# Low parts of all weights by subtraction on VectorE, and a shorter interval between the modulation's multiply-adds

## The chip, the cores and the metric

The kernel runs on one core of one Trainium2 chip. The metric is the device time of one execution in microseconds (us). Below, TensorE is also PE, VectorE DVE, ScalarE ACT, GpSimd POOL and SyncE SP, as the profile's rows have them.

## The reference, cut to what matters

One transformer layer on 512 tokens of width 2048, all in float32. What is computed must be seen only in outline:

```python
mod = silu(c) @ w_ada + b_ada                    # 6 vectors of 2048: sh1 sc1 gt1 sh2 sc2 gt2
h = rms_norm(x, norm1_g) * (1 + sc1) + sh1
proj = h @ w_in                                  # attention q k v, index q k w, recurrence r k v and low-rank parts
mixed = concat(sparse_attention(...), recurrence(...)) @ w_out
x = x + gt1 * mixed
h2 = rms_norm(x, norm2_g) * (1 + sc2) + sh2
ffn = (silu(h2 @ w_ffn_gate) * (h2 @ w_ffn_up)) @ w_ffn_down
x = x + gt2 * ffn
```

The modulation `mod` is a vector times a 2048 x 12288 matrix. `sh1` and `sc1` are needed at the start, `gt1` at the end of the output projection, `sh2` and `sc2` at the second norm, `gt2` at the end.

## The kernel before

**Split matmuls.** A matrix product is made of three matmuls in the float32r format: a weight tile is split into `whi`, its rounded value, and `wlo`, what the rounding left, and so are the activations; the products hi x hi, lo x hi and hi x lo are added up in PSUM. Three matmuls with 512 columns are one step, so TensorE has three passes over all weights.

**Jobs.** The weights stream in as jobs (lines 231 to 292). A job is a tile `wraw` of 128 x 1024 (512 KB), loaded by SyncE into one of 3 buffers by `issue_to`, which is called for the job three ahead. `split_to` makes `whi` and `wlo` of its two halves of 128 x 512, in 4 buffers each, so two jobs' worth: at the start of a job the halves of this job and the next are asked for, and from its middle one more. `run_jobs` writes the job's matmuls and yields after every third.

**The two ways of splitting.** `split` (line 196) has ScalarE cast the half to `whi`, and VectorE subtract it from the raw half to give `wlo`. In the stage between the first projection blocks and the output projection, where `state["mid"]` is set (line 1496), every second half goes another way (lines 259 to 263): ScalarE casts it, ScalarE writes the negated `whi` into `wlo`, and GpSimd issues a DMA that reads the same weights once more from HBM and adds them to `wlo`.

**What sets the order.** The order of the instructions on each engine is made when the program is built. Streams (generators) for the recurrence's preparation (`prep_stream`), the triangular solves (`solve(0)` on GpSimd, `solve(1)` on VectorE), the recurrence (`scan`), its end (`post_stream`), the sparse attention's index and top-k (`idx_stream`), the attention heads (`head_stream`) and the modulation (`ada_stream`) run beside the jobs; `drive` steps each of them after every third matmul. A planner's clock `clk`, built from rough costs of each instruction (lines 73 to 86), tells a stream when to go on: `until` waits on the planner's TensorE clock until a tile should be ready, and `room(engine, limit)` until the planned queue of an engine is no longer than the limit ahead of TensorE, in planned microseconds. Nothing of that clock is in the program: only the order that came out of it is.

**The modulation.** `ada_stream` (lines 974 to 1008) goes through 16 blocks (4 each for `gt1`, `sh2`, `sc2`, `gt2`) of 16 chunks. A chunk is a tile `wad` of 128 x 512 (256 KB), loaded by SyncE three chunks ahead. The first chunk of a block is scaled on ScalarE, the others are multiplied and added on VectorE (`scalar_tensor_tensor`, line 1006). At the end of a block VectorE transposes and reduces it to `part`, and after four blocks TensorE spreads `part` into `pc`. Chunks of the first twelve blocks, 192, follow one another by at least `PACE` = 4.2 of the planner's microseconds (lines 997 to 1000); the last four blocks start with the feed-forward. `norm2` (line 1349) writes nothing until the first twelve blocks are in the order: it waits for `done["ada"]` to be 12. Then come the sum of squares `pst`, the inverse root `rr`, its transpose `prb` and the first tiles of `h2`.

Of the kernel before, what the change touches and what calls it, by code (L numbers as in the profile page):

```python
# [8 lines left out]
F32 = mybir.dt.float32  # L9
F32R = mybir.dt.float32r  # L10
I32 = mybir.dt.int32
AF = mybir.ActivationFunctionType
OP = mybir.AluOpType
# [10 lines left out]
PAIRS = 8  # L24
# [24 lines left out]
def layer_kernel(ctx, tc, x, c, positions, w_ada, b_ada, norm1_g, w_in, q_norm_g, k_norm_g,  # L49
# [38 lines left out]
    class Queue:  # L88
# [3 lines left out]
        def __getattr__(self, op):  # L92
# [3 lines left out]
            def call(*args, **kw):  # L96
# [26 lines left out]
                if key2 != "pe":  # L123
                    for v in vals[1:]:
                        if nm(v) in psread:
# [4 lines left out]
    PE, V, A, P, SP = (Queue(e, k) for e, k in ((nc.tensor, "pe"), (nc.vector, "dve"), (nc.scalar, "act"),  # L130
                                                (nc.gpsimd, "pool"), (nc.sync, "dma")))

    def now():
        return clk["pe"]

    SLACK = 0.5
    PACE, PACE2 = 4.2, 3.0

    def until(*aps):

        t = max(ready.get(nm(a), 0.0) for a in aps) + SLACK
        while now() < t:
            yield

    def room(key="dve", lim=3.0):
        while clk[key] - now() > lim:
            yield
# [25 lines left out]
    def G(name="g", dt=F32):  # L173
        return gpool.tile([128, 512], dt, name=name, tag="g")
# [21 lines left out]
    def split(hi, lo, src, eng=None):  # L196
        A.copy(hi, src)
        (eng or V).tensor_tensor(lo, src, hi.bitcast(F32), op=OP.subtract)
# [34 lines left out]
    state = {"issued": 0, "split": 0, "mid": False, "ffn": False}  # L233
# [16 lines left out]
    def split_to(n):  # L250
        while state["split"] < min(n, len(subs)):
            j, u = subs[state["split"]]
            if j["i"] >= state["issued"]:
                return
            h = max(1, j["nk"] // 2)
            hi = wpool.tile([128, 512], F32R, name="whi", tag="whi", bufs=4)
            lo = wpool.tile([128, 512], F32R, name="wlo", tag="wlo", bufs=4)
            hv, lv = (t[:, 0:h * j["n"]].rearrange("p (k m) -> p k m", m=j["n"]) for t in (hi, lo))
            if state["mid"] and state["split"] % 2:
                A.copy(hv, j["raw"][:, u * h:(u + 1) * h])  # L260
                A.activation(lv, hv.bitcast(F32), AF.Copy, scale=-1.0)
                P.dma_start(lv, j["view"][:, j["k0"] + u * h:j["k0"] + u * h + h, j["c0"]:j["c0"] + j["n"]],
                            accum_op=OP.add)
            else:
                split(hv, lv, j["raw"][:, u * h:(u + 1) * h])
            j["hi"] += [hv[:, i, :] for i in range(h)]
            j["lo"] += [lv[:, i, :] for i in range(h)]
            state["split"] += 1
# [3 lines left out]
    def run_jobs(a, b, eng=SP, every=3):  # L272
        for i in range(a, b):
            j = jobs[i]
            while j["need"] is not None and not j["need"]():
                yield
            if j["before"] is not None:
                j["before"]()
            issue_to(i + 3, eng)
            split_to(j["s0"] + 4)  # L280
            n = 0
            half = None
            for kk, o, l, r, st, sp in j["mms"](j):
                if half is None and j["nk"] > 1 and kk >= j["nk"] // 2 and not j["whole"]:
                    half = 1
                    split_to(j["s0"] + 5)
                mm(o, l, r, st, sp)
                n += 1
                if n % every == 0:
                    yield  # L290
            if j["after"] is not None:
                j["after"]()
# [63 lines left out]
    done = {"ada1": 0, "prep": 0, "idx": 0, "topk": 0, "ada": 0, "hfree": 0, "rb": 0}  # L356
# [7 lines left out]
    for k1, n1 in BLOCKS:  # L364
        for kind in ("scale", "shift"):
            n = 4 // n1
# [72 lines left out]
    def ccol(k):  # L439
        return cact[:, k:k + 1]  # L440
# [533 lines left out]
    def ada_stream():  # L974
        blocks = [(n, o, b) for n, o in (("gt1", 2), ("sh2", 3), ("sc2", 4), ("gt2", 5)) for b in range(4)]
        chunks = [(bi, k) for bi in range(16) for k in range(KD)]
        tiles = {}

        def load(i):
            if i < len(chunks):  # L980
                bi, k = chunks[i]
                n, o, b = blocks[bi]
                t = G("wad")
                SP.dma_start(t, wav[:, k, o * D + b * 512:o * D + b * 512 + 512])
                tiles[i] = t

        nl = 0
        acc = None
        last = 0.0
        for i, (bi, k) in enumerate(chunks):  # L990
            while bi >= 12 and not state["ffn"]:
                yield
            while nl < min(i + 3, 192 if bi < 12 else 256):
                load(nl)
                nl += 1
            t = tiles.pop(i)
            while now() < last + (PACE if bi < 12 else PACE2):
                yield
            yield from until(t)
            yield from room("dve", 2.0)  # L1000
            last = now()
            if k == 0:
                A.activation(t, t, AF.Copy, scale=ccol(0))
                acc = t
                continue
            V.scalar_tensor_tensor(acc, t, ccol(k), acc, op0=OP.mult, op1=OP.add)
            if k == KD - 1:
                start(ada_sum(acc, *blocks[bi]))

    def ada_sum(acc, n, o, b):  # L1010
        yield from until(acc)
        part = parts[o % 2]
        yield from room("dve", 4.0)
        colsum(part[:, b * 16:b * 16 + 16], acc)
        if b < 3:
            return
        yield from until(part)
        yield from banks(1)
        pc = PS("pc")
        spread(pc[:, 0:16], part)  # L1020
        yield
        V.tensor_tensor(mod[n], pc[:, 0:16], v1[:, o * 16:o * 16 + 16], op=OP.add)
        if n == "sc2":
            V.scalar_tensor_tensor(gp2, mod[n], 1.0, v1[:, 112:128], op0=OP.add, op1=OP.mult)
        done["ada"] += 4
# [215 lines left out]
    def start(gen):  # L1241
        streams.append(gen)
# [218 lines left out]
    ada_issue()  # L1461
    drive(until(jobs[1]["raw"]))
    split_to(4)

    def first_need(b):
# [23 lines left out]
    start(post_stream(range(0, 8, 2)))  # L1489
    start(post_stream(range(1, 8, 2)))  # L1490
    start(ada_stream())
    start(idx_stream())
    start(head_stream())
# [71 lines left out]
```

## Time and profile before

| | |
|---|---|
| median of 3 runs | 2835.9 us (2832.57 to 2840.85) |
| the profiled execution, its own time | 2832.56 us |
| its span, first to last instruction | 2830.8 us |
| TensorE matmul busy | 2678.4 us |
| VectorE, ScalarE, GpSimd busy | 1396.9, 877.0, 438.1 us |
| mean granted TensorE clock | 0.970 |

The profile is of one execution. Busy time is the time in which an engine works on instructions; a wait is put down to the instruction that released it. The granted clock is in shares of full speed. The stages in the span: first projection blocks to about 142 us; the input projection with recurrence and attention beside it to about 1143; the output projection to 1335; the second norm to 1368; the feed-forward to the end.

### The profile page before, as it was taken

What the parts mean: (1) busy time and instruction counts of PE and PEld (TensorE: products, weight loads), DVE (VectorE), ACT (ScalarE), POOL (GpSimd) and SP (SyncE); (2) the same over time, 40 slices, a digit from 0 to 9 for tenths busy, and PEclk for the clock granted to TensorE, in tenths of its full rate; (3) what the DMA queues carried; (4) which work ended last, traced back from release to release, by engine and by line L of the source; (5) the groups of instructions that cost most, each with busy time, mean ns of one, the idle gap of its engine ahead of it and who ended that gap; (6) DMA issues with size and microseconds to landing.
All of it is one profiled execution on the core that took longest, in us unless ns stands there. A gap on an engine that the chain in (4) does not pass through costs nothing.

```text
span 2830.8 us, 35243 instructions
## 1 busy us (share of the span) xinstructions
PE 2678.4 (95%) x13343; PEld 2116.4 (75%) x13343; DVE 1396.9 (49%) x2304; ACT 877.0 (31%) x1577; POOL 438.1 (15%) x455
## 2 busy tenths in 40 slices
PE   7989988879999979998699999999999999999999
PEld 4567766657777757887488888888888888888887
DVE  3455555778657876655854533332333323333233
ACT  3244433323332334432332222222222222222222
POOL 2012267851113323210300000000000000000000
PEclk8999999889999989999799999999999999999999
DMA  9987888587867546545454433323333333333333
GB/s 323 308 229 194 208 191 214 149 204 177 222 170 205 130 123 156 158 164 174 135 185 164 156 97 97 97 94 100 97 97 97 97 97 97 97 97 97 97 97 112
DMA packets 411963, 424.76 MB, mean 150 GB/s; under 512 B 55226, under 2 KB 359168, under 8 KB 411792
## 3 DMA queue, kind: packets, MB, share of 16 engines
q1 hardware_dynamic: 381312, 387.78, 44.2%
q0 software_dynamic: 30336, 34.46, 7.6%
q8 instruction: 105, 1.72, 0.2%
q14 instruction: 66, 0.54, 0.1%
q10 hardware_dynamic: 144, 0.26, 0.0%
HBM read 386.77 MB, written 35.65 MB: 149 GB/s over the span
## 4 chain that ended last, share of the span: by engine, by line
PE 79%; DMA 7%; DVE 5%; issue 4%; SPq 2%; ACT 1%; POOL 1%; POOLq 0%; DVEq 0%; ACTq 0%
PE acc L127 68%; DMA wlo<-in_w_in_dram 3%; PE vacc L127 3%; DMA wraw<-in_w_in_dram 2%; PE po L127 2%; SPq L127 2%; PE p L127 2%; PE adaacc L127 1%; DMA wada<-in_w_ada_dram 1%; DVE work L127 1%; PE pl L127 1%; DVE wlo L127 1%; DVE score L127 1%; PE dot L127 0%; DMA xtok<-in_x_dram 0%
## 5 line engine op out<-in xcount | busy, mean ns | idle before, releaser
L127 DVE TENSOR_TENSOR wlo<-wraw,whi 128x512 fp32r<-128x512 f32 (+2 forms) x750 | 517.5, 695 | 1106.8 <-ACT whi L127 1097.5
L127 ACT CAST whi<-wraw 128x512 fp32r<-128x512 f32 (+2 forms) x860 | 518.0, 608 | 1393.6 <-PE acc L127 1200.6
L127 PE MATMUL acc<-hhi,wlo 128*128 128x512 f32 (+1 forms) x2256 | 892.8, 396 | 51.1 <-DMA wlo<-in_w_in_dram 45.7
L127 PE MATMUL acc<-hhi,whi 128*128 128x512 f32 (+1 forms) x2256 | 915.5, 406 | 6.9 <-ACT hhi L127 3.9
L127 PE MATMUL acc<-hlo,whi 128*128 128x512 f32 (+1 forms) x2256 | 888.9, 394 | 3.4 <-DVE hlo L127 3.4
L127 PEld LDWEIGHTS acc<-hhi,wlo 128*128 128x128 f32 (+1 forms) x2256 | 428.3, 190 | 152.3 <-DMA wlo<-in_w_in_dram 52.8
L127 PEld LDWEIGHTS acc<-hhi,whi 128*128 128x128 f32 (+1 forms) x2256 | 428.2, 190 | 127.7 <-issue 28.8
L127 PEld LDWEIGHTS acc<-hlo,whi 128*128 128x128 f32 (+1 forms) x2256 | 428.4, 190 | 96.1 <-DVE hlo L127 6.2
L127 PE MATMUL acc<-act,whi 128*128 128x512 f32 x1408 | 434.9, 390 | 0.0
L127 PEld LDWEIGHTS acc<-act,whi 128*128 128x128 f32 x1408 | 263.2, 188 | 53.9
L127 PE MATMUL acc<-act,wlo 128*128 128x512 f32 x704 | 274.0, 389 | 0.0
L127 POOL DMA_DIRECT2D wlo<-in_w_in_dram x109 | 126.6, 1161 | 451.0 <-ACT wlo L127 359.2
L127 DVE SCALAR_TENSOR_TENSOR wad<-wad,cact 128x512 f32<-128x512 f32 x240 | 195.1, 813 | 1.2
L127 PEld LDWEIGHTS acc<-act,wlo 128*128 128x128 f32 x704 | 132.1, 188 | 27.6
L127 PE MATMUL acc<-mhi,whi 128*128 128x512 f32 x256 | 100.4, 392 | 0.0
L127 PE MATMUL acc<-mhi,wlo 128*128 128x512 f32 x256 | 99.7, 389 | 0.0
L127 PE MATMUL acc<-mlo,whi 128*128 128x512 f32 x256 | 99.6, 389 | 0.0
L127 DVE SCALAR_TENSOR_TENSOR x<-acc,gt,x 128x512 f32<-128x512 f32 x80 | 57.3, 751 | 39.8 <-PE acc L127 39.8
L127 POOL TENSOR_TENSOR stmp<-X,N 128x504 f32<-128x504 f32 (+33 forms) x69 | 71.1, 1031 | 3.3
L127 ACT ACTIVATE wlo<-whi 128x512 fp32r<-128x512 f32 (+1 forms) x110 | 69.2, 629 | 3.5
L127 POOL TENSOR_TENSOR X<-X,stmp 128x504 f32<-128x504 f32 (+33 forms) x69 | 68.8, 997 | 5.4
L127 PE MATMUL vacc<-whi,hhi 128*128 128x512 f32 x128 | 55.1, 430 | 1.8 <-ACT whi L127 1.8
(259 smaller groups left out, 2194.1 us busy)
## 6 DMA issues: line engine op xcount, KB each, us to landing
wad<-in_w_ada_dram SPq DMA_DIRECT2D x256, 256.0 KB, 3.9
wraw<-in_w_in_dram SPq DMA_DIRECT2D x108, 512.0 KB, 5.5
wraw<-in_w_ffn_down_dram SPq DMA_DIRECT2D x88, 512.0 KB, 3.5
wraw<-in_w_ffn_gate_dram SPq DMA_DIRECT2D x84, 512.0 KB, 3.5
wraw<-in_w_ffn_up_dram SPq DMA_DIRECT2D x84, 512.0 KB, 3.5
wada<-in_w_ada_dram SPq DMA_DIRECT2D x128, 256.0 KB, 6.6
wlo<-in_w_in_dram POOLq DMA_DIRECT2D x107, 256.0 KB, 5.4
wraw<-in_w_out_dram SPq DMA_DIRECT2D x32, 512.0 KB, 3.5
```

The source lines that it names most:

```text
L127: return f(*args, **kw)
```

## The change

The second way of splitting goes: every half has its low part from a subtraction on VectorE. `PACE` goes from 4.2 to 2.4 of the planner's microseconds. The room that a multiply-add wants on VectorE was 2.0; it becomes 1.5 from the end of the recurrence's preparation (`done["prep"] == PAIRS`, 8) to the end of the top-k, and 3.5 at other times. `PACE2`, for the last four blocks, stays.

```diff
-    PACE, PACE2 = 4.2, 3.0
+    PACE, PACE2 = 2.4, 3.0
...
-            if state["mid"] and state["split"] % 2:
-                A.copy(hv, j["raw"][:, u * h:(u + 1) * h])
-                A.activation(lv, hv.bitcast(F32), AF.Copy, scale=-1.0)
-                P.dma_start(lv, j["view"][:, j["k0"] + u * h:j["k0"] + u * h + h, j["c0"]:j["c0"] + j["n"]],
-                            accum_op=OP.add)
-            else:
-                split(hv, lv, j["raw"][:, u * h:(u + 1) * h])
+            split(hv, lv, j["raw"][:, u * h:(u + 1) * h])
...
-            yield from room("dve", 2.0)
+            yield from room("dve", 1.5 if done["prep"] == PAIRS and not done["topk"] else 3.5)
```

## Rows read from the trace of the kernel before

**Rows 1.** The page's first part: engine, busy us, share, count of instructions.

```profile
PE 2678.4 (95%) x13343; PEld 2116.4 (75%) x13343; DVE 1396.9 (49%) x2304; ACT 877.0 (31%) x1577; POOL 438.1 (15%) x455
```

**Rows 2.** Stages: window, length, busy us (count) by engine, PEclk, DMA share, GB/s.

```profile
142.00:212.00 70.00, 61.18 (x263) 48.56 (x256) 37.85 (x68) 31.89 (x53) 10.68 (x9) 0.95 0.82 230
212.00:354.00 142.00, 134.05 (x705) 102.75 (x704) 78.45 (x125) 61.42 (x110) 36.58 (x34) 0.96 0.80 201
354.00:495.00 141.00, 117.64 (x561) 90.48 (x560) 75.92 (x89) 48.45 (x87) 94.72 (x100) 0.92 0.85 203
495.00:640.00 145.00, 117.80 (x542) 82.94 (x542) 104.25 (x139) 50.20 (x97) 93.68 (x95) 0.87 0.75 175
640.00:1010.00 370.00, 353.08 (x2354) 266.06 (x2353) 274.02 (x553) 117.66 (x224) 88.93 (x94) 0.98 0.69 181
```

**Rows 3.** What TensorE waited for over the span: us, times, longest.

```profile
PE acc L127 <- DMA wlo<-in_w_in_dram: 45.7, 15, 6.8
PE pc L127 <- DVE part L127: 27.2, 1, 27.2
PE pT L127 <- DVE work L127: 13.4, 4, 7.1
```

**Rows 4.** Timeline, 446 to 453 us: start, length, instruction, count, [idle before, releaser].

```profile
445.89 1.14 ACT L127 CAST whi<-wraw 128x512 fp32r<-128x512 f32 x2 [5.26 <-DMA wraw<-in_w_in_dram]
...
447.06 0.63 ACT L127 ACTIVATE wlo<-whi 128x512 fp32r<-128x512 f32 x1
...
447.99 1.20 POOL L127 DMA_DIRECT2D wlo<-in_w_in_dram  x1 [1.59 <-ACT wlo L127]
...
452.45 0.79 PE L127 MATMUL acc<-hhi,wlo 128*128 128x512 f32 x1 [5.65 <-DMA wlo<-in_w_in_dram]
```

**Rows 5.** Timeline at the second norm, VectorE's rows and then TensorE's.

```profile
1336.42 0.69 DVE L127 TENSOR_TENSOR ssum<-ssum,sqx 128x512 f32<-128x512 f32 x1 [0.76 <-ACT sqx L127]
1337.03 10.19 DVE L127 SCALAR_TENSOR_TENSOR wad<-wad,cact 128x512 f32<-128x512 f32 x13
...
1348.61 11.77 DVE L127 SCALAR_TENSOR_TENSOR wad<-wad,cact 128x512 f32<-128x512 f32 x15
...
1334.43 0.39 PE L127 MATMUL acc<-mhi,wlo 128*128 128x512 f32 x1
1361.99 0.31 PE L127 MATMUL pc<-part,cst 128*32 128x16 f32 x8 [27.17 <-DVE part L127]
...
1368.19 0.80 PE L127 MATMUL acc<-hhi,whi 128*128 128x512 f32 x1 [1.63 <-ACT hhi L127]
```

**Rows 6.** The page's costliest groups: count, busy us, mean ns, idle before.

```profile
L127 POOL DMA_DIRECT2D wlo<-in_w_in_dram x109 | 126.6, 1161 | 451.0 <-ACT wlo L127 359.2 <-PE acc L127 39.4 <-ACT R L127 20.3
```

**Rows 7.** VectorE's groups in 212 to 354 us, then in 354 to 495 us.

```profile
L127 DVE SCALAR_TENSOR_TENSOR wad<-wad,cact 128x512 f32<-128x512 f32 x23 | 17.5, 759 | 0.0
L127 DVE TENSOR_TENSOR wlo<-wraw,whi 128x512 fp32r<-128x512 f32 x19 | 13.2, 693 | 48.7 <-ACT whi L127 48.7
...
L127 DVE SCALAR_TENSOR_TENSOR wad<-wad,cact 128x512 f32<-128x512 f32 x18 | 21.1, 1174 | 0.0
L127 DVE TENSOR_TENSOR wlo<-wraw,whi 128x512 fp32r<-128x512 f32 x15 | 14.4, 961 | 52.7 <-ACT whi L127 52.7
```

**Rows 8.** Instructions on `wad` by stage: VectorE's and ScalarE's busy us (count), PEclk, DMA.

```profile
142.00:590.00 448.00, 56.23 (x59) 2.85 (x4) 0.93 0.77 193
590.00:1010.00 420.00, 33.80 (x45) 2.15 (x3) 0.97 0.74 188
1010.00:1204.00 194.00, 25.03 (x32) 1.44 (x2) 0.97 0.52 143
1204.00:1334.00 130.00, 20.61 (x25) 1.44 (x2) 1.00 0.49 164
```

**Rows 9.** What SyncE's queue waited for: us, times, longest.

```profile
SPq L127 <- DVE wlo L127: 1459.4, 321, 16.5
SPq L127 <- DVE wad L127: 45.0, 29, 11.9
```

## The prediction

> **What bounds the kernel now.** I read the shares of the engines first [rows 1]: TensorE (PE) is busy 95% of the span, VectorE (DVE) half of it. So TensorE is the bound, and only its idle stretches and its slow-clock stretches can be won. The table by stage [rows 2] says where these are: between 142 and 640 us TensorE is busy 430.7 of 498 us (61.18 + 134.05 + 117.64 + 117.80), 67 us idle, at a granted clock of 0.95, 0.96, 0.92 and 0.87. From 640 to 1010 us it is busy 353 of 370. The third view, what TensorE waits for [rows 3], names two waits that matter: 45.7 us in 15 waits for the low part `wlo` written by an adding DMA, and one single wait of 27.2 us for `part`, the result of the modulation's multiply-adds. VectorE's `work` costs 13.4 us more.
>
> Both large waits are touched by the change, so I looked at each on the timeline. At 452.45 us [rows 4] the raw weights have landed and ScalarE has cast both halves by 447.0; ScalarE negates the odd half from 447.06, GpSimd issues the DMA at 447.99, and TensorE resumes 4.5 us later, having waited 5.65. At the norm between the output projection and the feed-forward [rows 5] the last projection matmul starts at 1334.43 and the squares' sum `ssum` is ready at 1336.42 + 0.69 = 1337.11. But the modulation is behind: VectorE works off 13 and 15 of its multiply-adds back to back from 1337.03, and TensorE starts only at 1361.99.
>
> **The change, part by part.**
>
> *The adding DMAs go.* 109 GpSimd issues of 1161 ns [rows 6] and as many ScalarE negations, 0.63 us each [rows 4], leave. Both engines have room (31% and 15% busy [rows 1]), so by themselves they are worth nothing on the path. What is worth something is the latency. In rows 4 the odd half would be ready one subtraction after the negation's start: 447.06 + 0.8 = 447.9, which is 4.6 us before the DMA's, so 4.6 of that 5.65 us goes. I made the same subtraction at all 15 waits; the stretch from the negation to the resumption is 4.5 to 10 us and exceeds the wait plus 0.8 us at nearly all of them, which gives 44.6 of 45.7 us, if VectorE is free at that moment. In 495 to 640 us it will not be (below), and 9.6 us of these waits lie there, so I take 35 us. Bounds: 0, if raw weights or VectorE are late instead, and 45.
>
> *The subtractions come.* About 110 more on VectorE. One takes 693 ns in 212 to 354 us and 961 ns in 354 to 495 [rows 7], where GpSimd runs its own triangular solve: 76 us at the first price, 106 at the second, and about 84 with a third of them in the crowded stretch. VectorE must have this time idle beside TensorE. In 212 to 354 it is busy 78 of 142 us and gets 19 x 0.69 = 13 more; in 354 to 495, 76 of 141 and 17 x 0.96 = 16 more; in 495 to 640, 104 of 145 and 14 x 0.96 = 13 more; in 640 to 1010, 274 of 370 and 37 x 0.69 = 26 more [rows 2, 7]. (The count of odd halves is that of the issues in the stage; the even ones of a stage are as many.)
>
> *The multiply-adds come closer together.* PACE is counted on the planner's own TensorE clock, so it sets how much TensorE work lies between two multiply-adds in program order. [Rows 8] count them by stage (VectorE's, less one transpose of each finished block of 16, plus the first of a block, which ScalarE does). From 1204 to 1334 us, where TensorE never waits, there are 25 - 2 + 2 = 25 in 130 us, one per 5.2 us: 4.2 rounded up to the planner's steps. 2.4 by the same ratio is 3.0 us, 43 there. In 142 to 590 there are 59 - 3 + 4 = 60, one per 7.5 us; by pace alone 105, and with the looser limit of 3.5 and the new subtractions in the queue I take 92. In 590 to 1010 there are 45 - 3 + 3 = 45; here VectorE runs the second solve, the scan's copies and the top-k, the limit falls from 2.0 to 1.5, and I take 33 (bounds 20 and 55). In 1010 to 1204 there are 32 - 2 + 2 = 32, and I take 48. The sum by the norm is 92 + 33 + 48 + 43 = 216; the norm needs 192 (12 blocks of 16), and now 60 + 45 + 32 + 25 = 162 to 163 are done, so that 13 + 15 and a ScalarE step remain [rows 5]. With every low bound (60 + 20 + 32 + 33) it is 145, so this is likely and not sure. If it holds, TensorE's wait ends when `ssum` is ready: 1361.99 - 1337.2 = 24.8 us. Next late is then the norm's own chain to the first feed-forward matmul, 1368.19 - 1361.99 = 6.2 us, which stays.
>
> *What it costs earlier.* 28 multiply-adds move out of the gap and more move forward, into 142 to 590 above all: 92 - 60 = 32 more there, of 759 ns in the calm stretch and 1174 ns beside the solve [rows 7], 24 to 38 us. VectorE then has, in 354 to 495, 76 + 16 + about 14 x 1.17 = 108 us of work against 118 us of TensorE; in 495 to 640, 104 + 13 + about 8 x 1.17 = 126 against TensorE's 118. So in that one stage VectorE becomes the longer of the two, and elsewhere it stays below. Queued behind a multiply-add on VectorE are the next halves' subtractions and the recurrence's preparation (`work`, `pack`), for which TensorE already waits 13.4 us [rows 3]. The new delay has no row of its own: at least nothing, at most all the added work of 354 to 640 (16 + 16 + 13 + 9 = 54 us); I take the nearest row doubled, +13 us.
>
> The row for that price is the step from 693 to 961 ns, and from 759 to 1174, between a stage without and a stage with the solve on GpSimd [rows 7]. The Trainium skill, page "SBUF — State Buffer", section "Who interferes with whom", speaks against this edit: a VectorE instruction with two SBUF inputs contends with a GpSimd instruction that reads SBUF, and the loser is fully blocked. The added subtractions are of that kind. The trace agrees in kind; the mean loss is 0.27 and 0.42 us.
>
> *The transfers.* The DMA engines are 75 to 85% busy in 142 to 640 us [rows 2], and the modulation's loads move earlier while the adding DMAs, which read the same weights a second time, go. SyncE issues loads in order, and a multiply-add's load waits there for a free buffer: 45.0 us in 29 waits now [rows 9], with raw weights queued behind. I price this at nothing, since SyncE's main wait is still for the raw buffers to be read (1459.4 us), that is, for TensorE's own progress; at most it doubles.
>
> *The clock.* Clock below 1 in rows 2 is worth 0.05 x 70 + 0.04 x 142 + 0.08 x 141 + 0.13 x 145 = 39 us at full clock, some of it in idle time. The matmul after the stall in rows 4 takes 0.79 us, and the first after the norm's gap 0.80, against 0.39 before that gap [rows 5]: that is the lower of the two levels (1.2 and 2.4 GHz) after a stall. If half of the stalls go, I take 10 us back (0 to 25).
>
> **The sum.** The profiled execution took 2832.6 us, span 2830.8 and 1.8 around it: 2832.6 - 24.8 - 35 - 10 + 13 = 2775.8. The median of the runs shown is 3.3 us above it, so I forecast 2778.
>
> **Rivals.**
>
> 1. *Raw weights are next.* The waits for `wlo` only become waits for weights that have not landed. For it: rows 4 itself, where ScalarE sat idle 5.26 us for the raw tile. Against it: the raw tile was there 5.4 us before TensorE resumed, and the adding DMAs' traffic goes. It leaves the norm's gain and some 5 us: about 2805.
>
> 2. *The planner still holds the multiply-adds back.* The change would not do what its second half says. For it: 590 to 1010 has only 45, and the limit falls there to 1.5. Against it: 30 more are enough, and 1010 to 1334 alone can give that at the new pace. With 28 or so left at the norm nothing is won there: 2832.6 - 35 - 10 + 8 + 3 = 2799, about 2800.
>
> 3. *VectorE becomes the bound from 142 to 640 us*, and the kernel is slower. Added there are 59 subtractions (9 + 19 + 17 + 14, about 48 us) and at most 45 multiply-adds (105 - 60, about 43 us), 91 us, and VectorE's order is fixed. All of it on the path, less the 24.8 and 44.6 won: 2832.6 + 91 - 69 = 2854, about 2857. It decides from the point where over three quarters of the added work are exposed. For it: 126 against 118 in one stage, and the stretched durations. Against it: VectorE is idle 64, 65 and 41 us in the three stages from 212 us on.
>
> **How the numbers follow.** The forecast gets 0.60, rival 1 0.14, rival 2 0.11, rival 3 0.09, and 0.06 is left for gains and costs that cancel. Low end: 24.8 + 45 + 25 won and nothing paid, 2741. The high end takes in rivals 1 and 2 with the larger crowding cost: 2822. About 0.3% (8.5 us) is what a measurement of this kernel can tell from no change. Faster by more: 0.60 + 0.14 + 0.11 = 0.85; within: 0.06; slower by more: 0.09.
>
> **What would show it.** No adding DMA and no wait for one; the odd subtractions ending about 5 us before their matmuls; VectorE's busy share of 495 to 640 us near 90%; TensorE idle a few us, not 27, at the norm, with the multiply-adds of the first twelve blocks ended before it. I am wrong if TensorE's waits move to `whi` or `wlo` by VectorE with a like sum, or if the run of multiply-adds at the norm is still there.

## The result and the profile after

| | before | after |
|---|---|---|
| median of 4 runs | 2836.7 us | 2789.4 us (2786.7 to 2793.3) |
| ratio | | 0.983, 95% interval 0.982 to 0.985 |
| profiled execution, span | 2830.8 us | 2784.5 us |
| mean granted TensorE clock | 0.970 | 0.977 |

The kernel became 47 us faster; 58 were forecast, and the time lies in the range. VectorE took up 57 us of busy time, ScalarE and GpSimd gave up 71 and 97. The first part of the page of the changed kernel, beside [rows 1]:

```profile
PE 2675.0 (96%) x13343; PEld 2115.2 (76%) x13343; DVE 1454.2 (52%) x2414; ACT 805.8 (29%) x1467; POOL 341.0 (12%) x345
```

What TensorE waited for in it, the longest sums (us, times, longest); the two large waits of [rows 3] are gone, and what VectorE makes heads the list:

```profile
PE pT L127 <- DVE work L127: 22.5, 5, 8.5
PE pst L127 <- DVE sums L127: 12.4, 5, 3.7
PE acc L127 <- ACT whi L127: 8.6, 2, 5.2
PE ps L127 <- DMA xtok<-in_x_dram: 8.4, 1, 8.4
PE p L127 <- DVE ch L127: 5.1, 2, 2.8
```

The stages of [rows 2] in the changed kernel (window, length, busy us with count of PE, PEld, DVE, ACT and POOL, PEclk, DMA share, GB/s):

```profile
142.00:212.00 70.00, 69.17 (x313) 55.08 (x312) 52.21 (x89) 29.00 (x49) 2.78 (x3) 1.00 0.73 243
212.00:354.00 142.00, 133.76 (x715) 103.84 (x715) 99.33 (x158) 51.23 (x96) 14.84 (x17) 0.99 0.65 203
354.00:495.00 141.00, 119.78 (x569) 89.34 (x568) 107.63 (x121) 39.04 (x72) 106.81 (x103) 0.92 0.67 191
495.00:640.00 145.00, 126.23 (x641) 90.23 (x640) 113.21 (x179) 44.67 (x90) 56.95 (x60) 0.92 0.68 184
640.00:1010.00 370.00, 346.46 (x2225) 262.06 (x2224) 304.96 (x618) 90.20 (x182) 52.99 (x58) 0.94 0.51 154
```

At the norm (timeline, VectorE's row and then TensorE's; compare [rows 5]) nothing of the modulation stands any more between the sums `ssum` and the norm. From the start of the last projection matmul to the first of the feed-forward 8.45 us pass (1321.06 - 1312.61), where 33.76 passed before (1368.19 - 1334.43): 25.3 us won.

```profile
1314.54 0.69 DVE L127 TENSOR_TENSOR ssum<-ssum,sqx 128x512 f32<-128x512 f32 x1 [0.76 <-ACT sqx L127]
...
1312.61 0.39 PE L127 MATMUL acc<-mhi,wlo 128*128 128x512 f32 x1
1315.38 1.59 PE L127 MATMUL pst<-cst,ssum 128*128 128x1 f32 x8 [2.38 <-DVE ssum L127]
...
1321.06 0.79 PE L127 MATMUL acc<-hhi,whi 128*128 128x512 f32 x1 [1.63 <-ACT hhi L127]
```

The last projection matmul itself came 21.8 us earlier (1312.61 for 1334.43), and from the norm on the two kernels are level: 1462.6 us to the end before, 1463.4 after. So the whole change is 25 us at the norm and 22 us ahead of it.

The modulation's instructions by stage, as [rows 8]: VectorE's 104 in the first stage are 98 multiply-adds and 6 transposes, and from 1204 us there are none left before the norm.

```profile
142.00:590.00 448.00, 91.22 (x104) 5.04 (x7) 0.95 0.67 200
590.00:1010.00 420.00, 43.01 (x57) 2.92 (x4) 0.94 0.54 160
1010.00:1204.00 194.00, 23.91 (x32) 0.72 (x1) 1.00 0.38 123
1204.00:1334.00 130.00, 0.00 (x0) 0.72 (x1) 0.96 0.32 101
```

**Where the 22 us come from.** TensorE's waits from 142 us to the last projection matmul, added up by stage and by what released them, from the view of waits and the timeline:

| stage | before: all (adding DMA, VectorE) | after: all (VectorE) |
|---|---|---|
| 142 to 354 us | 16.6 (13.3, 1.9) | 8.8 (7.4) |
| 354 to 495 | 23.3 (19.9, 2.1) | 21.0 (17.5) |
| 495 to 640 | 27.2 (9.6, 17.2) | 18.7 (11.5) |
| 640 to 905 | 4.0 (0, 0) | 1.2 (0) |
| 905 to 1010 | 12.9 (0.3, 7.5) | 22.3 (19.5) |
| 1010 to the norm | 9.2 (2.6, 6.7) | 1.1 (0) |
| sum | 93.3 (45.7, 35.4) | 73.2 (55.9) |

The same stretch of time isn't the same work in both kernels, but the sums are. All 45.7 us of waits for adding DMAs went; 20.5 us of them came back as waits for VectorE and 8.4 as waits for ScalarE (7.1 before, 15.5 after). Of the 15.5, 8.6 are two waits for `whi`. ScalarE was not the cause of them: it sat idle 8.5 and 16.2 us ahead of both casts, because the raw weights had not landed.

```profile
371.33 1.14 ACT L127 CAST whi<-wraw 128x512 fp32r<-128x512 f32 x2 [8.54 <-DMA wraw<-in_w_in_dram]
372.00 0.50 PE L127 MATMUL acc<-hhi,whi 128*128 128x512 f32 x1 [3.46 <-ACT whi L127]
...
602.80 1.14 ACT L127 CAST whi<-wraw 128x512 fp32r<-128x512 f32 x2 [16.18 <-DMA wraw<-in_w_in_dram]
603.47 0.80 PE L127 MATMUL acc<-hhi,whi 128*128 128x512 f32 x1 [5.15 <-ACT whi L127]
```

Two stages gave the gain back. In 354 to 495 us the waits only changed their name. In 905 to 950 us a new hole opened; there the recurrence, the top-k, the norms of q and k and the multiply-adds meet on VectorE. Before, and then after (windows as above):

```profile
640.00:905.00 265.00, 260.97 (x1794) 196.07 (x1793) 187.53 (x368) 85.94 (x169) 55.51 (x64) 0.99 0.74 194
905.00:950.00 45.00, 45.00 (x330) 35.79 (x329) 35.81 (x82) 15.33 (x29) 11.35 (x11) 1.00 0.63 160
950.00:1010.00 60.00, 47.11 (x233) 34.19 (x234) 50.67 (x105) 16.40 (x28) 22.07 (x20) 0.91 0.51 136
```

```profile
640.00:905.00 265.00, 263.80 (x1766) 200.41 (x1765) 211.91 (x416) 70.52 (x141) 32.47 (x38) 1.00 0.54 161
905.00:950.00 45.00, 31.13 (x232) 24.74 (x230) 41.35 (x94) 6.64 (x15) 4.89 (x7) 0.66 0.49 152
950.00:1010.00 60.00, 51.52 (x231) 36.91 (x230) 51.70 (x109) 13.04 (x27) 15.63 (x13) 0.91 0.40 128
```

TensorE is idle 13.9 of those 45 us and the clock falls to 0.66, while VectorE is busy 41. The timeline of the changed kernel shows one of the holes: TensorE needs `ch`, a copy of 0.41 us, which stands in VectorE's queue behind top-k rounds and one multiply-add of 0.74 us.

```profile
939.36 0.74 DVE L127 SCALAR_TENSOR_TENSOR wad<-wad,cact 128x512 f32<-128x512 f32 x1
940.02 0.42 DVE L127 MAX8 m<-score 128x8 f32<-128x256 f32 x1
...
940.88 0.68 DVE L127 MAX8 m<-score 128x8 f32<-128x512 f32 x1
...
941.67 0.68 DVE L127 MATCH_REPLACE8 score<-m,score 128x512 f32<-128x512 f32 x1
942.27 0.41 DVE L127 COPY ch<-p 64x256 f32<-64x256 f32 x1
...
942.73 0.48 PE L127 MATMUL po<-ch 128*64 128x64 f32 x4 [2.97 <-DVE ch L127]
```

### The profile page after: what moved, and what is told of

The parts are those of the page before. It is cut to its first block, busy times and chain, and to the rows that moved or that the text cites. A ratio compares the mean times of both kernels' runs of the same rounds, so it can differ in the third digit from the quotient of the medians.

```text
span 2784.5 us, 35139 instructions
## 1 busy us (share of the span) xinstructions
PE 2675.0 (96%) x13343; PEld 2115.2 (76%) x13343; DVE 1454.2 (52%) x2414; ACT 805.8 (29%) x1467; POOL 341.0 (12%) x345
## 4 chain that ended last, share of the span: by engine, by line
PE 84%; DVE 7%; DMA 4%; issue 2%; SPq 1%; ACT 1%; POOL 1%; DVEq 0%; ACTq 0%; POOLq 0%
PE acc L127 72%; PE vacc L127 3%; PE po L127 2%; DMA wraw<-in_w_in_dram 2%; PE p L127 2%; SPq L127 1%; DVE wlo L127 1%; DVE wad L127 1%; PE adaacc L127 1%; DMA wada<-in_w_ada_dram 1%; PE pl L127 1%; PE dot L127 1%; DVE work L127 1%; ACT whi L127 0%; DVE score L127 0%
## 5 line engine op out<-in xcount | busy, mean ns | idle before, releaser
L127 DVE TENSOR_TENSOR wlo<-wraw,whi 128x512 fp32r<-128x512 f32 (+2 forms) x860 | 598.0, 701 | 1087.1 <-ACT whi L127 1082.3
L127 PE MATMUL acc<-hhi,whi 128*128 128x512 f32 (+1 forms) x2256 | 915.2, 406 | 13.2 <-ACT whi L127 8.6
L127 POOL TENSOR_TENSOR rn<-st,cst 128x8 f32<-128x8 f32 x16 | 32.1, 2007 | 232.5 <-DVE st L127 232.3
L127 PEld LDWEIGHTS acc<-mhi,wlo 128*128 128x128 f32 x256 | 48.1, 188 | 10.0
L127 PEld LDWEIGHTS acc<-mlo,whi 128*128 128x128 f32 x256 | 48.1, 188 | 9.8
```

The costliest lines, as they stand in the source:

```text
L127: return f(*args, **kw)
```

## The experiments

The theory after the result: the two halves of the change are two gains, at the norm and at the low parts, and VectorE's queue gives part of them back. Ratios are to the kernel before on the same chip, with 95% intervals; the changed kernel has 0.983 (0.982 to 0.985). A us figure worked out from a ratio takes 2837 us for the kernel before. The times of one chip stand up to 6 us from those of another, so between experiments ratios are compared.

### The two halves alone

```diff
# e1: from the changed kernel
-    PACE, PACE2 = 2.4, 3.0
+    PACE, PACE2 = 4.2, 3.0
...
-            yield from room("dve", 1.5 if done["prep"] == PAIRS and not done["topk"] else 3.5)
+            yield from room("dve", 2.0)
# e2: from the kernel before
-    PACE, PACE2 = 4.2, 3.0
+    PACE, PACE2 = 2.4, 3.0
...
-            yield from room("dve", 2.0)
+            yield from room("dve", 1.5 if done["prep"] == PAIRS and not done["topk"] else 3.5)
```

> The subtractions alone: all low parts by subtraction, the multiply-adds at the old interval of 4.2 and the old limit of 2.0. Theory (the change's two halves are two gains that add up: about 25 us at the norm, about 22 us from the low parts): no wait for an adding DMA, the wait of about 27 us at the norm stays, some 2812 us. Rival (the subtractions crowd VectorE and it is the earlier multiply-adds that won everything): 2830 us or more.

> The shorter interval alone: 2.4 and the limits 1.5 and 3.5, while every second low part is still made by the adding DMA. Theory: the wait at the norm goes (25 us), the 45 us of waits for adding DMAs stay, with a few us of crowding, about 2815 us. Rival (the two halves need one another, since the earlier multiply-adds and their loads delay the adding DMAs): 2830 us or more, with more than 60 us of waits for adding DMAs.

Measured: e1 2813.6 us, 0.993 (0.992 to 0.995); e2 2821.1 us, 0.996 (0.995 to 0.997). What TensorE waited for, first e1, then e2:

```profile
PE pc L127 <- DVE part L127: 28.0, 1, 28.0
PE pT L127 <- DVE work L127: 21.0, 5, 6.5
```

```profile
PE acc L127 <- DMA wlo<-in_w_in_dram: 36.0, 17, 6.4
PE pst L127 <- DVE sums L127: 9.4, 5, 3.6
```

e1 came out as the theory has it: the last projection matmul at 1315.8 us, 18.6 earlier than before, and the old wait at the norm. e2 has no wait for `part`, but its last projection matmul comes at 1346.9 us, 12.5 later than before: half of what the norm gives is paid ahead of it. The rival's way of paying is not it, since the waits for adding DMAs became shorter, 36.0 us for 45.7. All waits ahead of the norm are only 1.5 us longer than before. The rest is in TensorE's own busy time from 142 us to the last projection matmul, 1109.7 us for 1098.9, at a mean granted clock of 0.95 for 0.96; how much of that is the clock's these runs do not separate. And the two don't add up: 0.67% and 0.40%, where both together give 1.66%, some 17 us more. With low parts by subtraction the earlier multiply-adds cost nothing up to the norm (1312.6 us with an interval of 2.4, 1315.8 with 4.2); with adding DMAs they cost 12.5.

### What the added work costs where it stands

```diff
# e5: from the changed kernel
-            V.scalar_tensor_tensor(acc, t, ccol(k), acc, op0=OP.mult, op1=OP.add)
+            if bi >= 12 or k == KD - 1:
+                V.scalar_tensor_tensor(acc, t, ccol(k), acc, op0=OP.mult, op1=OP.add)
# e6: from the changed kernel
+            if state["mid"] and state["split"] % 2:
+                A.copy(hv, j["raw"][:, u * h:(u + 1) * h])
+                A.activation(lv, hv.bitcast(F32), AF.Copy, scale=-1.0)
+            else:
+                split(hv, lv, j["raw"][:, u * h:(u + 1) * h])
```

> The changed kernel without the multiply-adds of the first twelve blocks but the last one of each (168 of 180 on VectorE are left out; the loads stay): what they cost where they now stand. Theory (they are most of the crowding): waits for work, pack, sums and ch on VectorE fall by over half from about 55 us, 2770 us. Rival (they are hidden): 2786 us or more.

> The changed kernel with the odd low parts of the middle stage left as ScalarE's negated copy, so neither subtracted nor added by a DMA: what the 110 subtractions cost where they now stand. Theory (the crowding is shared): 2778 us. Rival (they are hidden): 2787 us or more. Rival (they are most of it): 2770 us or less.

Measured: e5 2753.0 us, 0.971 (0.968 to 0.973), so the multiply-adds of twelve blocks, 168 of them left out, cost 1.26%, 36 us, where they stand. e6 2761.3 us, 0.974 (0.971 to 0.976): the 110 odd subtractions, with ScalarE's negated copy in their place, cost 0.97%, 28 us. Neither is hidden, and the theory had both too low; by its time alone e6 meets the rival that the subtractions are most of the crowding, but e5 shows that the multiply-adds are more. Leaving instructions out also changes the planner's order of the rest, so both prices hold that too.

TensorE's waits ahead of the norm fall from 73.2 us to 47.4 and 58.0, those for VectorE from 55.9 to 37.5 and 47.1: by a third in e5, and not by over half as expected. Most of the fall is in 905 to 1010 us, where the waits for VectorE go from 19.5 us to 4.0 and 10.5. In 354 to 495 us they go from 17.5 only to 13.2 and 16.7. The largest wait for VectorE over the whole span, for `work` (22.5 us in the changed kernel), stands in both (e5, then e6), and in e1 too (21.0):

```profile
PE pT L127 <- DVE work L127: 21.4, 4, 6.4
PE pT L127 <- DVE work L127: 22.7, 5, 9.9
```

So neither the multiply-adds nor the odd subtractions alone make the wait for `work`. That it is the preparation's own chain of VectorE steps, which the waits for adding DMAs had covered (13.4 us before), is likely and not shown: no run leaves out both.

### Traffic or latency

```diff
# e7: from the changed kernel
+    scr = dram.tile([4, 128, 512], F32, name="scr")
...
             split(hv, lv, j["raw"][:, u * h:(u + 1) * h])
+            if state["mid"] and state["split"] % 2:
+                sc = scr[state["split"] // 2 % 4, :, 0:h * j["n"]].rearrange("p (k m) -> p k m", m=j["n"])
+                P.dma_start(sc, j["view"][:, j["k0"] + u * h:j["k0"] + u * h + h, j["c0"]:j["c0"] + j["n"]])
# e8: the same, but
+    scr = dram.tile([4, 128, 64], F32, name="scr")
...
+                P.dma_start(scr[state["split"] // 2 % 4], j["view"][:, j["k0"] + u * h, j["c0"]:j["c0"] + 64])
```

> The changed kernel with the adding DMAs' traffic put back without their latency: with every second half GpSimd issues a plain DMA that copies the same weights to scratch in HBM, which nobody reads. Theory (what went is the latency between cast and low part): 2789 to 2795 us, no new wait of over 10 us. Rival (what went is the traffic that kept the raw weights late): waits for raw weights and for casts grow, 2805 us or more.

> As e7, with the scratch copy cut to 64 columns of one weight row block (32 KB instead of 256): the same number of GpSimd issues, an eighth of the traffic. In e7 all was level with the changed kernel up to 972 us and the 20 us were lost after it, with waits for rr, sums and work. Theory (GpSimd's in-order queue and the order, not the traffic): most of e7's loss stays, 2800 us or more. Rival (the traffic): within 6 us of the changed kernel, 2789 us.

Measured: e7 2808.6 us, 0.990 (0.988 to 0.994), 20 us slower than the changed kernel, as the traffic rival had it. But e8, with an eighth of that traffic, is as slow: 2811.1 us, 0.991 (0.989 to 0.992). So it is not the traffic. What the two have in common is 109 more issues on GpSimd, 694 and 547 ns each:

```profile
L127 POOL DMA_DIRECT2D scr<-in_w_in_dram x109 | 71.4, 694 | 21.7 <-DMA scr<-in_w_in_dram 19.0 <-issue 1.5 <-DVE kf L127 0.6
```

```profile
L127 POOL DMA_DIRECT2D scr<-in_w_in_dram x109 | 59.3, 547 | 13.5 <-DMA scr<-in_w_in_dram 6.6 <-DMA wad<-in_w_ada_dram 4.5 <-issue 2.3
```

and that the planner, which puts 1.1 of its microseconds on GpSimd for each issue, makes another order of them. Waits in e7 grow by 17 us ahead of the norm, for VectorE mostly (65.3 for 55.9) and GpSimd (7.9 for 1.1). A third thing is the experiment's own: there are four scratch buffers, and GpSimd waits 19.0 and 6.6 us for earlier copies into them. Which of these it is stays open. That the adding DMAs of the kernel before paid a second price of this kind, which my sum did not have, is possible and not shown.

### The limit and the interval

```diff
# e3: from the changed kernel
-            yield from room("dve", 1.5 if done["prep"] == PAIRS and not done["topk"] else 3.5)
+            yield from room("dve", 2.0)
# e4, e9, e10: from the changed kernel
-    PACE, PACE2 = 2.4, 3.0
+    PACE, PACE2 = 3.2, 3.0      # e9: 2.8, e10: 3.6
```

> The changed kernel with the limit kept at 2.0 throughout. Theory (the interval does it, the limits only shift some multiply-adds): within 6 us of the changed kernel, 2784 to 2795 us. Rival (the limit of 1.5 during the scan and top-k protects TensorE): waits of the scan for VectorE grow by 10 us or more there, 2800 us.

> The changed kernel with an interval of 3.2. The multiply-adds of the first twelve blocks ended 190 us before the norm at 2.4, so 3.2 should still end them in time. Theory (closely queued multiply-adds are what crowds VectorE and costs some 10 us before 1010 us): about 2781 us, faster than the changed kernel by 5 to 10. Rival (the crowding comes from the subtractions or from the order): 2789 us as the changed kernel. If they do not end in time: a wait at the norm again, up to 2814 us.

> The changed kernel with an interval of 2.8, between 2.4 (2789 us) and 3.2 (2774 us). Theory (how closely the multiply-adds stand decides): 2778 to 2785 us. Rival (small differences of the order decide, no trend): anywhere in 2770 to 2795.

> The changed kernel with an interval of 3.6. At 3.2 the twelve blocks ended at 1236 us, 67 us before the last projection matmul. Theory (wider is better until they end too late): ended some 10 to 30 us before the norm, 2768 to 2775 us. Rival: multiply-adds are left at the norm, one 0.75 us wait each, 2780 us or more.

| | interval | us | ratio | last chunk of twelve blocks | last projection matmul |
|---|---|---|---|---|---|
| e3 | 2.4, limit 2.0 | 2788.1 | 0.984 (0.983 to 0.986) | 1208.8 us | 1312.6 us |
| after | 2.4 | 2789.4 | 0.983 (0.982 to 0.985) | 1123.9 | 1312.6 |
| e9 | 2.8 | 2781.0 | 0.980 (0.979 to 0.982) | 1210.1 | 1307.0 |
| e4 | 3.2 | 2774.5 | 0.979 (0.978 to 0.981) | 1235.9 | 1302.8 |
| e10 | 3.6 | 2763.4 | 0.974 (0.973 to 0.976) | 1287.0 | 1281.2 |

By the time, the two limits together are worth nothing at this interval (e3). What each of them does e3 doesn't show, since it changes both, and the waits did move: 32.9 us for 22.4 in 905 to 1010 us, 43.0 for 48.5 ahead of 640 us. With the changed limits the interval matters: each step wider is faster (the 95% intervals of neighbours up to 3.2 overlap). At 3.6 it is faster than either side had expected, though the last chunk just misses the last projection matmul, as the rival had it, and the wait for `part` is back, 7.8 us of it. In e10:

```profile
PE pT L127 <- DVE work L127: 25.4, 5, 8.9
PE ps L127 <- DMA xtok<-in_x_dram: 8.4, 1, 8.4
PE pc L127 <- DVE part L127: 7.8, 1, 7.8
```

The work is the same in all of these; it is only spread out further. TensorE's waits ahead of the norm are 73.2, 70.8, 63.3 and 54.2 us at 2.4, 2.8, 3.2 and 3.6.

But width alone doesn't decide. e3 has its last chunk as late as e9 and not its gain. And e1, with 4.2 and the limit of 2.0, comes to the last projection matmul at 1315.8 us, 34.6 later than e10. In 905 to 1010 us TensorE idles 36 us in e1 and 11 in e10, though the two have 17 and 18 chunks there (e1, then e10; windows as above):

```profile
905.00:1010.00 105.00, 68.78 (x347) 50.02 (x346) 92.82 (x213) 14.60 (x27) 15.11 (x15) 0.75 0.33 101
905.00:1010.00 105.00, 94.31 (x484) 72.54 (x485) 83.03 (x185) 29.91 (x70) 26.25 (x29) 0.87 0.40 126
```

So the limits or the order of the rest count as well; 3.6 with the old limit, and 4.2 with the changed ones, were not run.

### The crowded stage, and both together

```diff
# e11: from the changed kernel
-            yield from room("dve", 1.5 if done["prep"] == PAIRS and not done["topk"] else 3.5)
+            while done["prep"] == PAIRS and not done["topk"]:
+                yield
+            yield from room("dve", 3.5)
# e12: from the changed kernel
-            while now() < last + (PACE if bi < 12 else PACE2):
+            while now() < last + (PACE2 if bi >= 12 else 2.4 if done["topk"] else 3.2 if done["prep"] == PAIRS else 3.6):
...
-            yield from room("dve", 1.5 if done["prep"] == PAIRS and not done["topk"] else 3.5)
+            yield from room("dve", 0.5 if done["prep"] == PAIRS and not done["topk"] else 3.5)
```

> The changed kernel with no multiply-add queued between the end of the preparation and the end of the top-k, where VectorE stood full at 905 to 950 us and TensorE's clock fell to 0.62. Theory (the multiply-adds there cost the 10 us that were lost): those waits and the fall shrink, the rest still fits before the norm (about 90 chunks in 1000 to 1310 us), 2778 us. Rival (the subtractions and the top-k itself fill VectorE there): 2787 us or more. If the rest doesn't fit: a wait at the norm of up to 25 us.

> The changed kernel with the interval by stage: 3.6 until the preparation's end, 3.2 with a limit of 0.5 until the end of the top-k, 2.4 after it. It joins what the intervals of 3.6 (2763 us, 7.8 us still waited for the modulation at the norm) and the empty top-k stage (2771 us) won. Theory (both gains are the room that VectorE has in the crowded stages): no wait for the modulation at the norm, 2750 to 2760 us. Rival (what is won in the crowded stages is lost among the attention heads after the top-k, where the multiply-adds now stand closest): 2765 us or more.

Measured: e11 2771.1 us, 0.977 (0.976 to 0.979), 18 us faster than the changed kernel, more than expected. The stretch of 905 to 950 us in it:

```profile
905.00:950.00 45.00, 37.23 (x256) 28.63 (x256) 38.41 (x92) 9.08 (x18) 4.08 (x7) 0.81 0.23 68
```

TensorE is idle 7.8 us there for 13.9, at a clock of 0.81 for 0.66. Its waits for VectorE fall from 12.2 us to 3.7; another 3.7 us is one wait that the view puts down to "issue", so to nothing that the profile shows. From 905 to 1010 us all waits fall from 22.4 us to 7.9. So the multiply-adds made most of the hole. e12 has 2761.6 us, 0.974 (0.972 to 0.977), between theory and rival and level with e10, so what it gains over e11 it does not gain over an even 3.6. No wait for `part` is left in it; its last projection matmul comes at 1291.1 us, 9.9 later than in e10, where 7.8 us are then waited for `part`. By the ratios e10 and e12 are 26 us faster than the changed kernel and 73 us faster than the one before.

## Why the prediction was right, and where it was off

**The norm: right in kind and size.** Forecast 24.8 us, measured 25.3. The count of multiply-adds was right in its sum only: I had 92, 33, 48 and 43 chunks by stage, of which 192 were needed; there are 105 (98 and 7 on ScalarE), 57, 30 and none. The looser limit let more through in the first stage than I took (in e3, with 2.0, 87). The 57 lie above my bound of 55, in the stage where the new hole opened. In e10 the last of them come 5.8 us after the last projection matmul starts, so the whole gain is there at 2.4, 2.8 and 3.2, and most of it at 3.6.

**The adding DMAs' latency: right in kind, taken too low.** I took 35 of 45.7 us for fear of a busy VectorE in 495 to 640 us; all of it went. The stage that I had for the dearest was not: VectorE is busy 113 of 145 us there, 78% and not near 90. Its instructions are shorter there than before (a subtraction 792 ns for 936), and the solve on GpSimd has moved ahead: GpSimd is busy 57 us there, for 94 with the DMA issues before, and 107 for 95 in the stage before it.

**The cost of the crowding: this is the term that failed.** I took +13 us, in 354 to 640 us, from TensorE's waits for `work`. Measured are +20.5 us of waits for VectorE and +8.4 for ScalarE, less 3.9 for GpSimd, and 0.6 of others: +25.6. In 354 to 495 us I had VectorE's work right to a microsecond (108 forecast, 107.6 measured) and concluded that 108 against 118 of TensorE leaves it off the path. It did not: 17.5 us of waits for VectorE stand there, in place of 19.9 for the DMAs. A busy share of 76% says how much is to be done, and not when the one result comes that TensorE needs; and by e5 and e6 most of these waits stay when either half of the added work goes. The other place, 905 to 1010 us, I had not looked at, because the changed limit of 1.5 seemed to guard it. Waits for VectorE rose there from 7.5 us to 19.5, and e5 and e11 show that the multiply-adds cost there.

**The transfers: priced at nothing, and not nothing.** SyncE's waits for `wad` buffers stayed near what they were (50.8 us for 45.0), but TensorE's waits for `whi` ahead of the norm rose from 3.1 us to 8.6, both times behind raw weights that came late. Why these were late the runs do not show.

**The clock: nothing back.** I took 10 us. The waits account for 20.1 of the 21.8 us, so 1.7 are left for the clock and all else; TensorE's busy time between 142 us and the last projection matmul is 2.1 us shorter (1096.8 for 1098.9). The clock rose where waits went (0.96 to 0.99 in 212 to 354 us, 0.87 to 0.92 in 495 to 640) and fell in the new hole (0.98 to 0.94 in 640 to 1010 us).

So ahead of the norm 32 us were forecast, 35 + 10 - 13, and 21.8 measured: -45.7 + 25.6 - 1.7 with the signs of the sum. That is 10 of the 11 us between the forecast and the time. And it is partly luck that they are so few: 10.7 us more were won from the adding DMAs than I took, and 12.6 more were paid in new waits. Two slips in the working are small. The sum with its 3.3 us gives 2779, not 2778. And in [rows 4] the raw tile was there 6.6 us before TensorE resumed; 5.4 us is from the end of the casts.

**The rivals.** Raw weights were next in a small part: they stand behind the 8.6 us of waits for `whi`, of the 45.7 that went. The planner did not hold the multiply-adds back. The third, VectorE as the bound, did not come: it had 91 us on the path between 142 and 640 us, and the waits for VectorE rose there by 15.2 (21.2 to 36.4). By e5 and e6 multiply-adds and subtractions do cost 36 and 28 us where they stand, but what the multiply-adds cost in the kernel before was not measured in the same way.

**The shared port.** A subtraction takes 1036 ns in 354 to 495 us, where the solve runs, and 792 in the next stage, where less of it does; 961 and 936 before. VectorE's groups of the changed kernel in the two stages:

```profile
L127 DVE TENSOR_TENSOR wlo<-wraw,whi 128x512 fp32r<-128x512 f32 x31 | 32.0, 1036 | 27.0 <-ACT whi L127 27.0
...
L127 DVE TENSOR_TENSOR wlo<-wraw,whi 128x512 fp32r<-128x512 f32 x30 | 23.6, 792 | 27.5 <-ACT whi L127 27.4
```

With 691 ns in 142 to 354 us this is the stretch that [rows 7] show. The Trainium skill, "SBUF — State Buffer", section "Who interferes with whom", names its kind, a VectorE instruction with two SBUF inputs beside a GpSimd instruction that reads SBUF; that the port is its cause no run here shows by itself.

## What to carry to other kernels

A filler that runs beside the main work need not be done early: the same 192 steps at 3.6 instead of 2.4 were worth 26 us here, and a due time missed by 6 us made the gap at the norm 6 us longer (14.4 for 8.45). How wide is best has to be tried: e1, at 4.2 and with the old limit, came to the last projection matmul no earlier than the changed kernel. Before work is moved onto an engine that is busy for most of a stage (VectorE was busy 36 of the 45 us from 905 on in the kernel before), look for the short instruction on that engine that the bound engine waits for, and count what will stand in the queue ahead of it; the busy share doesn't tell. A step with a long latency, such as a DMA that adds, should be priced by the time between its inputs and its reader, not by its engine's time.

## What the runs showed of the hardware

109 GpSimd DMA issues that nobody reads slowed the kernel by 20 us, and as much at 32 KB as at 256 KB each, though GpSimd is busy only 14% of the span in both; whether GpSimd's queue, its waits for the scratch buffers or the planner's other order is behind it stays open. And a TensorE that waits for VectorE in small pieces loses more than the pieces: in 905 to 950 us it was busy 31 of 45 us and the granted clock was 0.66, between the lower level of 1.2 GHz and the full 2.4.
